# Low parts of value and output weights added up by DMA, and the modulations taken out of the first folded part, in a two-layer decoder trunk

## The chip, the cores and the metric

One core of one Trainium2 chip runs the whole program. The metric is the device time of one execution in microseconds, as the median of the timed runs. TensorE (PE) multiplies, VectorE (DVE), ScalarE (ACT) and GpSimd (POOL) work on tiles of 128 partitions, and SyncE (SP) does nothing but issue DMAs, in the order of its queue.

## The reference

```python
for i in range(DEPTH):                                   # DEPTH = 2, D_MODEL = 1024, SEQ = 512
    mod = silu(c) @ ada_w[i] + ada_b[i]                  # 6 x 1024 modulations
    sh_t, sc_t, gt_t, sh_f, sc_f, gt_f = split(mod, 6)
    h = rmsnorm(x, norm_tok_g[i]) * (1.0 + sc_t) + sh_t
    y = retention_mixer(h, ...) if i % 2 == 0 else mlstm_mixer(h, ...)
    x = x + gt_t * y
    h = rmsnorm(x, norm_ffn_g[i]) * (1.0 + sc_f) + sh_f
    x = x + gt_f * conv_ffn(h, ...)                      # (silu(a) * b) @ w_down, a, b = conv(h @ w_up), D_FF = 2816
return rmsnorm(x, final_g)
```

Both mixers have four heads. A head projects `h` to queries, keys, values (512 wide) and gates, weighs its scores (retention by a fixed decay table, mLSTM by a row that comes from the gates), attends, normalises its result over the 512 values, and multiplies it by the output weights into `x`. All of it is float32.

## The kernel before, in words

`x` and `h` are held transposed, as 8 tiles of 128 features x 512 positions. A float32 product is made of three products of TensorE's reduced type: high x high, high x low and low x high (`mm3`, lines 281 to 283). So every chunk of weights, 128 x 1024 float32 or 512 KB, is loaded by SyncE into a raw buffer `raw` (`Chunk`, line 182; six buffers, `RAWS`), ScalarE casts its high part `whi` (line 164), and VectorE subtracts to get the low part `wlo` (line 169). Both have eight buffers (`WBUFS`). The raw buffer comes free when the low part is made, and only then can SyncE's queue pass the load that takes this buffer next: it is the sixth `raw` load after it.

`low_part_added` (lines 172 to 177) is another way to the low part: ScalarE writes -`whi` into `wlo` (line 175), and a DMA that GpSimd issues adds the raw chunk to it (line 176). Then VectorE has no part in it, and the raw buffer is free once the DMA has landed. Before, only the folded part of the FFN uses it: for the chunk `wa`, the sums `ws` and every second `wt`, 86 DMAs in the two layers.

The program is a list of items (a projection, a piece of attention, a norm), each with the chunks that it uses (`Use`). The last loop of `trunk` goes through it: ahead of each item it loads, casts and splits the chunks of up to four items further on (`Ahead`), then emits the item, then some side work. A scheduler places the instructions on the engines' queues; each queue, SyncE's included, then runs in order. For each layer the items are those of `heads` (line 876): the projections of a head's queries and keys, its values (`v_items`, four chunks a head), its scores (S), gates (g) and attention (A), the middle and the end of its normalisation, and its output pieces (`pieces`, `contract_items`, four chunks a head), with the heads interleaved. `boundary` (line 629) takes the last output pieces in two halves of the positions, with the next norm beside them; then follows the FFN.

What the heads need besides weights comes over SyncE's queue too: the retention's decay table `tab` (line 1091) and the mLSTM's rows `mb` and `db` (lines 1307 and 1308). From `mb` VectorE and ScalarE make the weights of the scores (lines 1314 to 1318).

The FFN's upper part is `folded`, 17 folds in a written order, one `unit(i)` each: products of TensorE with the work for the next unit between them, and the down projection of earlier groups, whose chunks (`Beside`, line 199) lie in two side buffers.

Side work are the modulations: `gemv` (line 136) loads a tile `ada` of 128 x 1025 into one of the two side buffers (line 139), and one VectorE operation multiplies and sums it (line 140). 48 of them run behind the items of mixer 0, as far as `LATER` allows, eight inside the folded part of layer 0 (load at line 525, operation in the next unit), and the others behind every second item later.

Of the kernel before, what the change touches and what calls it, by code (L numbers as in the profile page):

```python
# [15 lines left out]
P = 128  # L16
T = 512
# [11 lines left out]
RAWS = 6  # L29
LATER = 32  # L30
FOLD_FROM = 5
WPAD = 64
OFF = 16
# [37 lines left out]
def trunk(ctx: ExitStack, tc: tile.TileContext, xT, cb, pos, vec, decay, zmask, ada, w_s0, w_in0, w_v0,  # L71
          w_o0, w_in1, w_v1, w_o1, w_up, w_dn, out):
    nc = tc.nc
# [105 lines left out]
    class Chunk:  # L179
# [6 lines left out]

        def low(self):
            self.lo = low_part(self.raw, self.hi, self.r, self.off)

# [162 lines left out]
    class Use:  # L352


        def __init__(self, src, n, off=0):
            self.src, self.n, self.first, self.off = src, n, None, off

# [8 lines left out]
    class Ahead:  # L366
# [26 lines left out]
        def low(self):  # L393
            self.flat[self.at_low].chunk.low()
            self.at_low += 1
# [12 lines left out]

    def folded(folds, h, terms, pairs, downs, modulate):

        no = lambda *a: None
        banks, sums, other = {}, {}, []

# [24 lines left out]
        def unit(i):  # L440
# [50 lines left out]
            if f:  # L491
                f.high_24()
                f.low_24(i % 2)
                if other:
                    layer, m, after, raw = other.pop()
                    gemv(layer, m, raw)
                    after()
            else:
                ahead.high()
                ahead.high()  # L500
# [20 lines left out]
            load_down(i + 2)  # L521
            if modulate and side and i % 2 == 0 and i + 2 < len(folds):
                layer, m, after = side.pop(0)
                raw = aside("ada")[:]
                nc.sync.dma_start(raw, ada[layer, m])
                other.append((layer, m, after, raw))
            if i == len(folds) - 2:
# [42 lines left out]
    def v_items(w_v, hd, h, v, split, between=lambda j: None):  # L570
        pss = []

        def mk(j):
            def fn(w):
                if j == 0:
                    pss.extend(bank("pv") for _ in range(4))
                for t in range(4):
                    for kk in range(2):
                        k = 2 * j + kk
                        cs, ws = slice(t * P, t * P + P), slice(kk * T, kk * T + T)  # L580
                        st, sp = k == 0, k == KT - 1
                        PE.matmul(pss[t][:], h[k].hi[:, cs], w[0].hi[:, ws], start=st, stop=False)  # L582
                        PE.matmul(pss[t][:], h[k].hi[:, cs], w[0].lo[:, ws], start=False, stop=False)  # L583
                        PE.matmul(pss[t][:], h[k].lo[:, cs], w[0].hi[:, ws], start=False, stop=sp)  # L584
                if j == 3:
                    for t in range(4):
                        split(v, pss[t])
            return fn
        for j in range(4):
            item([Use(w_v[hd, j], 2 * T)], mk(j))  # L590
            between(j)
# [22 lines left out]
    def pieces(src, n, gate, ys):  # L614
# [3 lines left out]
        def piece(i):  # L618
            def run(w, t0, t1, after=lambda m: None, js=None, lead=False):
                contract_tiles(w, n, gate, ys, i, t0, t1, after, js, lead)  # L620
            return Use(src(i), per * n * P), run
        return [piece(i) for i in range(KT // per)]
# [6 lines left out]
    def boundary(late, last, norm):  # L629


        for u, _ in late + last:
            u.off = OFF
        for p, after in ((0, lambda m: norm.square(0, m)), (1, norm.later)):
# [280 lines left out]
    class Ffn:  # L915
# [77 lines left out]
        def items(self, norm):  # L993
# [3 lines left out]
            downs = [p for gi in range(len(GROUPS) - 1) for p in self.down(gi)]  # L997
            steps, run = folded(folds, self.h, self.start.terms, pairs, downs, self.layer == 0)

# [398 lines left out]
    for n, (uses, fn, free) in enumerate(items):  # L1398
# [7 lines left out]
        if n < bars[0]:  # L1406
            for _ in range(2 if n > 20 and n % 10 == 0 else 1):
                if len(side) > LATER:
                    side_work(*side.pop(0))
# [107 lines left out]
```

## Time and profile before

| | us |
|---|---|
| median of 3 timed runs | 1559.96 (1559.96 to 1562.13) |
| the profiled execution | 1554.46 |
| its span in the profile | 1552.7 |
| TensorE's granted clock, mean | 0.992 |

Busy shares of the span are 97% for TensorE, 77% for VectorE, 55% for ScalarE and 15% for GpSimd; the DMA engines moved 241.79 MB, 156 GB/s in the mean.

How to read the lines further down: a group gives line, engine, operation, output <- inputs, the number of instructions, then their busy time, the mean ns of one, and the engine's idle time ahead of them with what ended most of it. A line of the waits gives who waited for whom, the sum in us, how often, and the longest. A line of the chain or of a timeline gives start and duration in us, the engine, the line and the tile; "SPq" is SyncE's queue, which stands for the issue of a DMA. Times count from the start of the span.

### The profile page before, as it was taken

How to read it: one execution, taken by the hardware profiler on the slowest of the kernel's cores; microseconds unless marked ns; L12 is line 12 of the kernel's file. 1: busy time of each engine (PE TensorE's matmuls, PEld its weight loads, DVE VectorE, ACT ScalarE, POOL GpSimd, SP SyncE). 2: the span in 40 equal slices, each digit the busy share in tenths (PEclk: the TensorE clock that was granted, in tenths of full speed). 3: DMA queues.
4: the chain of work that ended last, by engine and by line, in shares of the span. 5: the costliest groups of instructions: out<-in, count | busy, mean ns of one | idle time of the engine just before them, and what ended most of it. 6: DMA issues, size and time to landing. Idle time of an engine off the chain costs nothing. (4 is left out here: it accounts for less than half of the span.)

```text
span 1552.7 us, 23173 instructions
## 1 busy us (share of the span) xinstructions
PE 1513.2 (97%) x8996; PEld 1337.2 (86%) x8996; DVE 1200.5 (77%) x1814; ACT 861.2 (55%) x1282; POOL 229.3 (15%) x242
## 2 busy tenths in 40 slices
PE   7999999999999999999999999999999999999997
PEld 4788888888988999998988878888889889999997
DVE  8985768786997878887777777777588977787775
ACT  4534524443456767676655554554545666767763
POOL 3421001110130111111110011001022201111102
PEclk9999999999999999999999999999999999999999
DMA  8753464655315888887444433443312258777751
GB/s 312 228 186 109 143 188 159 204 177 167 110 42 136 210 208 205 230 195 202 160 128 149 149 109 105 152 144 112 126 54 72 67 135 198 195 191 188 187 140 55
DMA packets 72224, 241.79 MB, mean 156 GB/s; under 512 B 9761, under 2 KB 12065, under 8 KB 72114
## 3 DMA queue, kind: packets, MB, share of 16 engines
q1 hardware_dynamic: 59730, 195.22, 38.4%
q0 software_dynamic: 12384, 45.09, 15.3%
q8 instruction: 70, 1.15, 0.3%
q14 instruction: 40, 0.33, 0.1%
HBM read 193.06 MB, written 2.12 MB: 126 GB/s over the span
## 5 line engine op out<-in xcount | busy, mean ns | idle before, releaser
L164 ACT CAST whi<-raw 128x1024 fp32r<-128x1024 f32 (+1 forms) x190 | 194.3, 1029 | 144.4 <-PE pp L282 58.3
L169 DVE TENSOR_TENSOR wlo<-raw,whi 128x1024 fp32r<-128x1024 f32 (+1 forms) x158 | 191.5, 1219 | 46.7 <-ACT whi L164 46.1
L281 PE MATMUL pp<-hh,whi 128*128 128x512 f32 x560 | 218.4, 390 | 2.3 <-DVE vl L278 2.0
L282 PE MATMUL pp<-hl,whi 128*128 128x512 f32 x560 | 218.1, 390 | 0.0
L283 PE MATMUL pp<-hh,wlo 128*128 128x512 f32 x560 | 218.0, 389 | 0.0
L595 DVE SCALAR_TENSOR_TENSOR x<-po,mod,x 128x512 f32<-128x512 f32 (+1 forms) x184 | 114.2, 629 | 71.6 <-PE po L283 68.0
L282 PE MATMUL po<-ggl,whi 128*128 128x512 f32 (+1 forms) x448 | 154.0, 345 | 0.0
L283 PE MATMUL po<-ggh,wlo 128*128 128x512 f32 (+1 forms) x448 | 153.5, 344 | 0.0
L281 PE MATMUL po<-ggh,whi 128*128 128x512 f32 (+1 forms) x448 | 153.0, 345 | 0.0
L422 PE MATMUL p<-hh,whi 128*128 128x256 f32 x544 | 150.6, 277 | 0.0
L423 PE MATMUL p<-hl,whi 128*128 128x256 f32 x544 | 150.4, 276 | 0.0
L424 PE MATMUL p<-hh,wlo 128*128 128x256 f32 x544 | 150.4, 276 | 0.0
L140 DVE SCALAR_TENSOR_TENSOR ada<-ada,c_ext 128x1025 f32<-128x1025 f32 x93 | 115.7, 1245 | 32.3 <-DMA ada<-ada 32.2
L281 PEld LDWEIGHTS pp<-hh,whi 128*128 128x128 f32 x560 | 105.2, 188 | 24.6 <-DVE vl L278 2.5
L283 PEld LDWEIGHTS pp<-hh,wlo 128*128 128x128 f32 x560 | 105.2, 188 | 21.8
L282 PEld LDWEIGHTS pp<-hl,whi 128*128 128x128 f32 x560 | 105.2, 188 | 21.4
L281 PE MATMUL po<-yh,whi 128*128 128x256 f32 (+1 forms) x352 | 115.8, 329 | 0.0
L282 PE MATMUL po<-yl,whi 128*128 128x256 f32 (+1 forms) x352 | 115.6, 328 | 0.0
L283 PE MATMUL po<-yh,wlo 128*128 128x256 f32 (+1 forms) x352 | 115.6, 328 | 0.0
L927 ACT ACTIVATE cv<-p,vecs 128x512 f32<-128x512 f32 x68 | 53.1, 780 | 96.2 <-PE p L424 57.3
L932 DVE SCALAR_TENSOR_TENSOR cv<-p,vecs,cv 128x511 f32<-128x511 f32 (+1 forms) x136 | 101.0, 745 | 2.2
L422 PEld LDWEIGHTS p<-hh,whi 128*128 128x128 f32 x544 | 102.2, 188 | 0.1
(287 smaller groups left out, 3986.9 us busy)
## 6 DMA issues: line engine op xcount, KB each, us to landing
ada<-ada SPq DMA_DIRECT2D x96, 512.5 KB, 4.0
raw<-w_in SPq DMA_DIRECT2D x62, 512.0 KB, 3.8
wb<-w_up SPq DMA_DIRECT2D x34, 512.0 KB, 4.4
wa<-w_up SPq DMA_DIRECT2D x34, 512.0 KB, 5.3
wlo<-wa POOLq DMA_DIRECT2D x34, 512.0 KB, 4.6
wlo<-ws POOLq DMA_DIRECT2D x34, 512.0 KB, 4.9
raw<-w_o SPq DMA_DIRECT2D x32, 512.0 KB, 3.5
raw<-w_dn SPq DMA_DIRECT2D x32, 512.0 KB, 4.4
```

What stands on the lines that cost most here:

```text
L140: return V.scalar_tensor_tensor(raw, raw, 1.0, c_ext[:], op0=ALU.mult, op1=ALU.mult, accum_out=mods[layer][:, f : f + 1])
L164: A.copy(hi, w[:, r])
L169: V.tensor_tensor(lo, w[:, r], hi.bitcast(F32), op=ALU.subtract)
L281: PE.matmul(o, ah, bh, start=start, stop=False)
L282: PE.matmul(o, ah, bl, start=False, stop=False)
L283: PE.matmul(o, al, bh, start=False, stop=stop)
L422: PE.matmul(o, hi[:, ch], b[0], start=st, stop=False, skip_group_check=True)
L423: PE.matmul(o, hi[:, ch], b[1], start=False, stop=False, skip_group_check=True)
L424: PE.matmul(o, lo[:, cl], b[0], start=False, stop=sp, skip_group_check=True)
L595: V.scalar_tensor_tensor(x[m][:, r], ps[:, r], gate_col, x[m][:, r], op0=ALU.mult, op1=ALU.add)
L927: A.activation(acc[:], ps[:], AF.Identity, bias=col("fcb", self.layer * 2 * FT + f), scale=self.conv_col(f, 2))
L932: V.scalar_tensor_tensor(acc[:, s:], ps[:, : T - s], self.conv_col(f, j), acc[:, s:], op0=ALU.mult, op1=ALU.add)
```

## The change

It does three things.

1. The values' chunks (`w_v0` of heads 1 to 3, all of `w_v1`) and the output pieces (`w_o0`, `w_o1`) get `added`, and their low parts are made by `low_part_added`. The pieces inside `boundary` don't. That is 12 + 16 + 2 x 10 = 48 chunks.
2. The eight modulations inside the folded part of layer 0 go, with the code for them.
3. `LATER` is 24 rather than 32, and every fifth item beyond the 20th rather than every tenth has two modulations behind it, so that mixer 0 takes 56 of them.

```diff
--- before.py
+++ after.py
@@ -27,7 +27,7 @@
 WCOLS = 1024
 WBUFS = 8
 RAWS = 6
-LATER = 32
+LATER = 24
 FOLD_FROM = 5
 WPAD = 64
 OFF = 16
@@ -184,8 +184,8 @@
         def high(self):
             self.hi = high_part(self.raw, self.r, self.off)
 
-        def low(self):
-            self.lo = low_part(self.raw, self.hi, self.r, self.off)
+        def low(self, added=False):
+            self.lo = (low_part_added if added else low_part)(self.raw, self.hi, self.r, self.off)
 
         def lo_at(self, at, k):
             return at * P
@@ -352,8 +352,8 @@
     class Use:
 
 
-        def __init__(self, src, n, off=0):
-            self.src, self.n, self.first, self.off = src, n, None, off
+        def __init__(self, src, n, added=False, off=0):
+            self.src, self.n, self.first, self.off, self.added = src, n, None, off, added
 
     def item(uses, fn, free=True):
         for u in uses:
@@ -391,7 +391,8 @@
             self.at_high += 1
 
         def low(self):
-            self.flat[self.at_low].chunk.low()
+            u = self.flat[self.at_low]
+            u.chunk.low(u.added)
             self.at_low += 1
     ahead = Ahead()
 
@@ -406,12 +407,12 @@
             then(ps)
         item([Use(src, KT * P)], fn)
 
-    def folded(folds, h, terms, pairs, downs, modulate):
+    def folded(folds, h, terms, pairs, downs):
 
 
 
         no = lambda *a: None
-        banks, sums, other = {}, {}, []
+        banks, sums = {}, {}
 
         def product(i, n, o, start=False):
             hi, hc, lo, lc = folds[i].p[n]
@@ -491,10 +492,6 @@
             if f:
                 f.high_24()
                 f.low_24(i % 2)
-                if other:
-                    layer, m, after, raw = other.pop()
-                    gemv(layer, m, raw)
-                    after()
             else:
                 ahead.high()
                 ahead.high()
@@ -519,11 +516,6 @@
             if i + 2 < len(folds):
                 folds[i + 2].load()
             load_down(i + 2)
-            if modulate and side and i % 2 == 0 and i + 2 < len(folds):
-                layer, m, after = side.pop(0)
-                raw = aside("ada")[:]
-                nc.sync.dma_start(raw, ada[layer, m])
-                other.append((layer, m, after, raw))
             if i == len(folds) - 2:
                 for _ in range(4):
                     ahead.load()
@@ -587,7 +579,7 @@
                         split(v, pss[t])
             return fn
         for j in range(4):
-            item([Use(w_v[hd, j], 2 * T)], mk(j))
+            item([Use(w_v[hd, j], 2 * T, True)], mk(j))
             between(j)
 
     def add_residual(ps, m, gate_col, t0=0, t1=T):
@@ -618,7 +610,7 @@
         def piece(i):
             def run(w, t0, t1, after=lambda m: None, js=None, lead=False):
                 contract_tiles(w, n, gate, ys, i, t0, t1, after, js, lead)
-            return Use(src(i), per * n * P), run
+            return Use(src(i), per * n * P, n == 4), run
         return [piece(i) for i in range(KT // per)]
 
     def contract_items(ps, between=lambda i: None):
@@ -630,7 +622,7 @@
 
 
         for u, _ in late + last:
-            u.off = OFF
+            u.off, u.added = OFF, False
         for p, after in ((0, lambda m: norm.square(0, m)), (1, norm.later)):
             for n, (u, run) in enumerate(late):
                 item([u], lambda w, run=run, p=p, n=n: run(w[0], *HALVES[p], lead=p + n == 0), False)
@@ -995,7 +987,7 @@
             folds = [Fold((w[f], w[f + FT])) for f in range(FOLD_FROM, FT)]
             pairs = [self.steps(f) for f in range(FOLD_FROM, FT)]
             downs = [p for gi in range(len(GROUPS) - 1) for p in self.down(gi)]
-            steps, run = folded(folds, self.h, self.start.terms, pairs, downs, self.layer == 0)
+            steps, run = folded(folds, self.h, self.start.terms, pairs, downs)
 
             def early(n):
                 todo = [steps.pop(0) for _ in range(n)]
@@ -1404,7 +1396,7 @@
         if not uses or not free or n <= 6:
             continue
         if n < bars[0]:
-            for _ in range(2 if n > 20 and n % 10 == 0 else 1):
+            for _ in range(2 if n > 20 and n % 5 == 0 else 1):
                 if len(side) > LATER:
                     side_work(*side.pop(0))
         elif side and n % 2:
```

In the order of the instructions VectorE has 48 `wlo` subtractions less, ScalarE 48 `ACTIVATE wlo<-whi` more, GpSimd 48 `DMA wlo<-raw` more, and SyncE the same number of DMAs, 61 of them at another place. TensorE's instructions are the same ones in nearly the same order. On SyncE's queue `tab` of retention's head 0 moves ahead of the fourth w_o0 load, which it stood behind; `tab` of head 3 stands behind the load of a w_o0 chunk that takes the buffer of an added one; and the loads of two more modulations come shortly before the first boundary.

**Head 1 of the mLSTM mixer.** First SyncE's queue, where `mb` and `db` of this head stand behind two w_v1 loads; in rows "raw" and a number is a load into a raw buffer. Before:

```order
L182 DMA raw_1663_9314<-w_in1 128x1024
L182 DMA raw_1669_9351<-w_in1 128x1024
L139 DMA ada_1657_9276<-ada 128x1025
L182 DMA raw_1681_9381<-w_v1 128x1024
L182 DMA raw_1693_9461<-w_v1 128x1024
L1307 DMA mb_1577_8886<-scratch_575 128x512
L1308 DMA db_1578_8887<-scratch_575 128x512
```

and after:

```order
L182 DMA raw_1663_9348<-w_in1 128x1024
L139 DMA ada_1627_9128<-ada 128x1025
L182 DMA raw_1669_9385<-w_in1 128x1024
L139 DMA ada_1657_9310<-ada 128x1025
L182 DMA raw_1681_9415<-w_v1 128x1024
L182 DMA raw_1693_9496<-w_v1 128x1024
L1299 DMA mb_1577_8916<-scratch_575 128x512
L1300 DMA db_1578_8917<-scratch_575 128x512
```

The load raw_1693 takes the buffer of raw_1633 in both, the sixth load ahead of it and the fourth w_o1 chunk of head 0. `mb` stands right behind it in both; a modulation's load has moved between the two w_in1 loads. What makes that buffer free has changed; on GpSimd's queue stand, after the change, `zs` and `zv` (the sums for the normalisation of head 0) and the DMAs of the four w_o1 chunks:

```order
L832 TENSOR_TENSOR zs_1536_8728<-z_1529_8681,z_1531_8696 128x512
L833 TENSOR_TENSOR zs_1537_8729<-z_1533_8711,z_1535_8726 128x512
L176 DMA wlo_1619_9064<-raw_1617_9060 128x1024
L176 DMA wlo_1624_9098<-raw_1622_9094 128x1024
L176 DMA wlo_1630_9135<-raw_1628_9131 128x1024
L832 TENSOR_TENSOR zv_1555_8822<-zq_1551_8814,zq_1552_8816 128x512
L833 TENSOR_TENSOR zv_1556_8823<-zq_1553_8818,zq_1554_8820 128x512
L176 DMA wlo_1635_9169<-raw_1633_9165 128x1024
```

Before, the two `zv` rows followed the `zs` rows directly, and no DMA stood on this queue here. The fourth DMA, of raw_1633, now has both `zv` sums ahead of it.

**A little later on VectorE**, where the normalisation of head 0 ends (`grs` is the root of the variance, `z` the head's result, `yl` a low part of what goes into the output product). Before:

```order
L296 RECIPROCAL grs_1605_8975<-grs_1605_8975 128x512
L1355 TENSOR_TENSOR z_1529_8652<-z_1529_8652,grs_1605_8975 128x512
L1355 TENSOR_TENSOR z_1531_8667<-z_1531_8667,grs_1605_8975 128x512
L1355 TENSOR_TENSOR z_1533_8682<-z_1533_8682,grs_1605_8975 128x512
L1358 SCALAR_TENSOR_TENSOR yl_1607_8981<-z_1529_8652,vecs_108,yh_1606_8980 128x512
L1355 TENSOR_TENSOR z_1535_8697<-z_1535_8697,grs_1605_8975 128x512
L1358 SCALAR_TENSOR_TENSOR yl_1609_8986<-z_1531_8667,vecs_108,yh_1608_8985 128x512
L169 TENSOR_TENSOR wlo_1671_9355<-raw_1669_9351,whi_1670_9353 128x1024
```

and after:

```order
L296 RECIPROCAL grs_1605_9005<-grs_1605_9005 128x512
L169 TENSOR_TENSOR wlo_1671_9389<-raw_1669_9385,whi_1670_9387 128x1024
L1347 TENSOR_TENSOR z_1529_8681<-z_1529_8681,grs_1605_9005 128x512
L1347 TENSOR_TENSOR z_1531_8696<-z_1531_8696,grs_1605_9005 128x512
L1347 TENSOR_TENSOR z_1533_8711<-z_1533_8711,grs_1605_9005 128x512
L1350 SCALAR_TENSOR_TENSOR yl_1607_9011<-z_1529_8681,vecs_108,yh_1606_9010 128x512
L1347 TENSOR_TENSOR z_1535_8726<-z_1535_8726,grs_1605_9005 128x512
```

The low part wlo_1671 of a w_in1 chunk, which stood behind the four `z` rows, now stands ahead of them, right behind `grs`.

**The end of the folded part of layer 0, SyncE's queue.** `wa` and `wb` are the last folds' chunks, "raw" of w_dn04 those of the down projection of the last group. Before:

```order
L525 DMA ada_1243_6941<-ada 128x1025
L222 DMA wb_1242_6938<-w_up 128x1024
L223 DMA wa_1241_6937<-w_up 128x1024
L139 DMA ada_1420_8073<-ada 128x1025
L182 DMA raw_1263_7104<-w_dn04 128x768
L182 DMA raw_1264_7106<-w_dn04 128x768
L182 DMA raw_1265_7108<-w_dn04 128x768
L139 DMA ada_1431_8140<-ada 128x1025
L182 DMA raw_1266_7110<-w_dn04 128x768
```

and after:

```order
L222 DMA wb_1219_6793<-w_up 128x1024
L223 DMA wa_1218_6792<-w_up 128x1024
L139 DMA ada_1420_8099<-ada 128x1025
L222 DMA wb_1243_6963<-w_up 128x1024
L223 DMA wa_1242_6962<-w_up 128x1024
L139 DMA ada_1431_8166<-ada 128x1025
L182 DMA raw_1263_7126<-w_dn04 128x768
L182 DMA raw_1264_7128<-w_dn04 128x768
```

The row of line 525, the load of the last folded modulation, is gone, and both `ada` loads of line 139 now stand ahead of all w_dn04 loads, where the second one stood between them.

## The prediction

> **What bounds the kernel now.** I read the busy times first, then TensorE's waits, then the chain of waits, and then the queues around each wait.
>
> ```profile
> span 1552.7 us, 23173 instructions
> PE 1513.2 (97%) x8996; PEld 1337.2 (86%) x8996; DVE 1200.5 (77%) x1814; ACT 861.2 (55%) x1282; POOL 229.3 (15%) x242
> L169 DVE TENSOR_TENSOR wlo<-raw,whi 128x1024 fp32r<-128x1024 f32 (+1 forms) x158 | 191.5, 1219 | 46.7 <-ACT whi L164 46.1
> ```
>
> TensorE is busy for 1513.2 of 1552.7 us, and the change leaves its products as they are. So all that can be won is its idle time, 39.5 us, and all that can be lost is new idle time or a lower clock. VectorE at 77% is not the bound: less work there pays only where TensorE waits for it. These are those waits (us in total, times, longest); the first start-up waits (line 1175 and its neighbours) the change doesn't touch.
>
> ```profile
> PE pms L291 <- ACT ssh L277: 5.2, 3, 2.0
> PE p L424 <- DMA wlo<-wt: 2.1, 1, 2.1
> PE pp L281 <- DVE vl L278: 2.0, 1, 2.0
> PE pvar L291 <- DVE vl L278: 1.3, 1, 1.3
> PE pav L282 <- DVE sl L278: 0.6, 2, 0.4
> PE pden L291 <- ACT o L1328: 0.5, 1, 0.5
> PE pav L281 <- ACT sh L277: 0.3, 1, 0.3
> ```
>
> No row says that TensorE's projections wait for a `wlo` of value or output weights. That is the first finding: the 48 subtractions that the change takes from VectorE end in time today. The gain can only be indirect, and so can the loss.
>
> **The edits themselves.** 48 subtractions of 1.219 us leave VectorE, 58.5 us. In their place come 48 multiplications on ScalarE and 48 DMAs issued by GpSimd. The folded parts show both today:
>
> ```profile
> 720.13 1.06 ACT L175 ACTIVATE wlo<-whi 128x1024 fp32r<-128x1024 f32 x1
> L176 POOL DMA_DIRECT2D wlo<-wa x34: 850/859/1051, 464.9 to 1487.0; - x34
> DMA to landing us min/median/max: 4.4/4.8/10.2
> ```
>
> ScalarE gets 48 x 1.06 = 51 us (55% becomes 58%), GpSimd 48 x 0.86 = 41 us (15% becomes 17%). Neither becomes a bound. A low part is now ready 1.06 + 4.8 = 5.9 us after its cast, at worst 1.06 + 10.2 = 11.3, where it was 1.22. A chunk is loaded up to four items ahead of its use, and that hides the delay from TensorE. The nearest row is that of the folded parts: of their 86 added chunks (34 `wa`, 34 `ws`, 18 `wt`) one is waited for, 2.1 us. At that rate 48 chunks cost from 0 to 1.2 us; I take zero, since that one DMA has a cause of its own (term 2). Without the cover each would cost about 5. But the raw buffer is held that much longer too, and SyncE's queue is in order: whatever stands behind a load that waits for this buffer is late. That is where I look for the price. The eight modulations that leave the folded part of layer 0 are loads and VectorE operations of 1.2 us, which now stand in mixer 0.
>
> **Term 1, head 1 of the mLSTM mixer: a loss.** The chain of waits (start, duration) of before runs through exactly such a buffer:
>
> ```profile
> 915.13 0.60 DVE zv L842
> 915.73 1.15 DVE wlo L169
> 916.89 0.33 SPq L182
> 917.31 5.69 DMA mb<-scratch
> ...
> 939.67 3.37 DVE grs L296
> 943.06 1.90 DVE z L1355 x3
> ...
> 947.00 1.28 ACT L1328
> 948.29 0.61 ACT o L1328
> 948.94 0.51 PE pden L291
> ```
>
> The `wlo` of 915.73 is that of the fourth w_o1 chunk. Its end frees the buffer for the w_v load (raw_1693 in the order), and directly behind that load in SyncE's queue stands `mb`, the row that head 1's score weights need. All that follows up to `pden` is serial, and `pden` already waits 0.5. After the change this chunk is one of the added ones. What sets its DMA:
>
> ```profile
> 912.98 1.05 ACT L164 CAST whi<-raw 128x1024 fp32r<-128x1024 f32 x1 [1.41 <-PE pv L584]
> 910.51 1.30 POOL L840 TENSOR_TENSOR zv<-zq,zq 128x512 f32<-128x512 f32 x1 [6.27 <-issue]
> 911.77 2.28 POOL L841 TENSOR_TENSOR zv<-zq,zq 128x512 f32<-128x512 f32 x1
> ```
>
> The cast waits for TensorE, so it stays at 912.98 to 914.03. The multiplication ends at 915.1. GpSimd has the two `zv` sums ahead of it (they end at 914.05, and up to 1.7 later, because a multiplication now stands between the squares and two DMA issues ahead of the sums). So the DMA goes out at 915.1 to 915.7 and lands 4.4 to 4.8 later, at 919.5 to 920.5, where the subtraction ended at 916.86: `mb` is 2.7 to 3.7 late, I take 3.2. In VectorE's order the `wlo` of raw_1669 now stands ahead of the `z` products where it stood behind them (946.80 below): 1.2 more before `o`.
>
> ```profile
> 946.80 1.22 DVE L169 TENSOR_TENSOR wlo<-raw,whi 128x1024 fp32r<-128x1024 f32 x1
> 437.00:440.00 3.00, 0.97 (x9) 0.77 (x8) 3.00 (x7) 0.81 (x2) 0.00 (x0) 1.00 0.39 152
> 440.00:444.00 4.00, 4.00 (x24) 4.00 (x23) 3.89 (x6) 1.84 (x5) 1.34 (x2) 0.57 0.00 0
> ```
>
> That is +4.4, a stall of about 5 us. The last two rows are stretches of before (duration, then busy times and counts by engine, then the clock): at the boundary at 437 TensorE idles 2.0, and then runs at a mean clock of 0.57 for 4 us. The lost 43% of 4 us are 1.7 us. The waits of 2.1 (735) and 2.0 (`pp` for `vl`) have no such stretch behind them, so 2 us is the edge, and 5 us should be well past it: +1.7. Bounds: without the late `wlo` and without the clock, with the quickest landing, +2.7; with a landing of 7, a second low stretch and the `wlo`, +9; if VectorE's relief lets the cast and the sums come early, +1 at the least.
>
> The Trainium skill ("TensorE: Matmul & The Clock Gate", Part 1: The HAM clock gate) has the clock fall after one idle window of about 3.4 us. The 2.0-us wait at 437 fell short of that and the clock fell all the same, so here the row decides; by either, 5 us is enough.
>
> The same skill ("DMA: Bandwidth & Descriptors", Anatomy of one DMA, SWDGE path) fits a GpSimd DMA as 2.0 us and the bytes at 436 GB/s; for 512 KB I estimate 3.2 us by that page, against the 4.8 median that lands in this trace. By the page `mb` would be about 1.5 us less late and the whole forecast 1.5 us lower; I keep the row.
>
> **Term 2, the end of the folded part of layer 0: a gain.** TensorE's wait of 2.1 for `wlo<-wt` is that of one DMA:
>
> ```profile
> L176 POOL DMA_DIRECT2D wlo<-wt x1: 859/859/859, 727.2 to 727.2; - x1
> DMA to landing us min/median/max: 4.5/5.2/10.2
> ...
> 727.47 0.33 SPq L139 DMA_DIRECT2D ada<-ada  x1
> 729.70 9.58 SPq L182 DMA_DIRECT2D raw<-w_dn  x5
> ```
>
> Issued at 727.2, it landed after 10.2 us, since a modulation's load of 512 KB went out 0.27 later, and five w_dn loads from 2.5 later. That load waited for the buffer of the last folded modulation (726.2 to 727.4 on VectorE). In the order after the change both `ada` loads stand before the w_dn loads and wait for no folded modulation, so the DMA should land in the median. The wait goes: -2.1; if the w_dn loads alone are enough to slow it, 0.
>
> **Terms 3 to 6, small ones.** (3) Head 0 of retention: `tab` moves ahead of one raw load on SyncE's queue and the wait at its `pav` shrinks, -0.4 of the 0.9 that the two `pav` rows give for heads 0 and 3. (4) Head 3: `tab` there stands behind a raw load whose buffer an added chunk frees, about as in term 1, but with a modulation's load beside it that waits longer today: +0.8, at most +3. (5) The boundary of mixer 0: two more modulations stand shortly before it on VectorE (2 x 1.2 us against 1.9 us idle in 408 to 418, 3.37 and 4.74 busy of 10): +0.5.
>
> ```profile
> 408.00:412.00 4.00, 4.00 (x38) 4.00 (x37) 3.37 (x6) 2.15 (x6) 1.92 (x2) 1.00 0.42 131
> 412.00:418.00 6.00, 5.92 (x52) 5.72 (x51) 4.74 (x13) 3.19 (x8) 0.88 (x1) 1.00 0.37 118
> 782.56 1.21 DVE L169 TENSOR_TENSOR wlo<-raw,whi 128x1024 fp32r<-128x1024 f32 x1
> 785.56 1.21 DVE L169 TENSOR_TENSOR wlo<-raw,whi 128x1024 fp32r<-128x1024 f32 x1
> ```
>
> (6) The boundary before mixer 1: three `wlo` of w_v1 (782.56 to 785.56, the first and last of three) leave VectorE beside the norm, but three multiplications enter ScalarE ahead of its squares: -0.5, from -2 to +1. The `vl` wait of 2.0 at the last value chunk stays (a modulation moves ahead of it, +0.2), and the one of 1.3 nets to zero: four `wlo` less on VectorE, as many multiplications on ScalarE ahead of the casts that `vl` needs.
>
> **Sum:** 4.4 + 1.7 - 2.1 - 0.4 + 0.8 + 0.5 - 0.5 + 0.2 = +4.6. The profiled execution took 1554.46, its span of 1552.7 and 1.76 around it, 5.5 less than the median of the timed runs, 1559.96. 1554.46 becomes 1559.1, and on the median's scale I predict **1564.6**.
>
> **The rivals.**
> (a) VectorE's relief wins, the end on the other side. Its place are the rows in which TensorE waits for `vl` and the norms: the `wlo` of w_v1 stood on VectorE ahead of `vl` and of the norm's sums. If those waits go (2.0 + 1.3, and 2.0 of the 5.2 at `pms`), term 2 and 3 come as above (-2.5), and `mb` is late by 2.7 with no lower clock, the sum is -5.1: 1554.9. It decides from the point at which the relief gives more than the 6.1 of term 1, less 2.5. For it: 58.5 us less on VectorE, the largest edit here. Against it: the same stretches get ScalarE work ahead of the casts that these chains need as well. 23%.
> (b) Both sides cancel: `mb` late by 2.7 and the clock stays, no late `wlo`, the rest as in the sum (-1.5): +1.2, 1561.2. For it: waits of 2.0 and 2.1 that left the clock alone. 28%.
> (c) The forecast, 1564.6. 37%.
> (d) The longer-held buffers hurt in more places: `tab` of head 3 is +3 rather than +0.8, the norm of mixer 0 gets all of the 2.4 us, and term 1 meets a landing near 7 (+2.5): +11.1 or 1571. Against it: before `mb` of heads 2 and 3 the buffer of the load ahead is that of a chunk whose low part VectorE still makes, before and after. 11%.
> (e) The change doesn't do what it says. In the order all 48 chunks have their new rows, and no engine has other work; 1%, at 1560.
>
> **How the numbers follow.** What a measurement can tell from no change is 0.2%, 3.1 us: faster is under 1556.8, slower over 1563.1. (a) is nearly all faster, 0.22; (b) and (e) and the low edge of the forecast are the same, 0.31; the rest, 0.47, slower. The range leaves out the outer part of (d) and the low tail of (a): 1555 to 1571; the forecast's own range is 1561 to 1568.
>
> **What would show it.** Term 1: in the chain of waits of after, `mb` lands near 926 rather than 923 and the step before it is a DMA `wlo`, not a VectorE `wlo`; `pden` waits about 5 us and a stretch of about 0.5 of the clock follows. Term 2: no row `p L424 <- DMA wlo<-wt`. Term 5: the first `pms` wait over 2.0. I am wrong if `mb` is issued at 917 again (its DMA landed early or the buffer wasn't the one), or if the `vl` rows vanish.

## The result and the profile after

| | before | after |
|---|---|---|
| median of the timed runs, us | 1560.15 (1559.96 to 1562.13) | 1577.36 (1576.63 to 1582.02) |
| the profiled execution | 1554.46 | 1577.51 |
| its span | 1552.7 | 1575.4 |

The ratio is 1.0114, with an interval of [1.0093, 1.0135]: 17.2 us slower. The direction was forecast, the size was not: 1564.6 was predicted, and 1577.4 lies outside the range of 1555 to 1571.

The page of after, and below it TensorE's waits that answer to those shown of before (the rows of the start, `pst`, come to 11.0 before and 11.8 after):

```profile
span 1575.4 us, 23311 instructions
PE 1520.0 (96%) x8996; PEld 1339.1 (85%) x8996; DVE 1145.9 (73%) x1766; ACT 908.2 (58%) x1330; POOL 263.8 (17%) x290
```

```profile
...
PE pav L281 <- ACT sh L277: 7.5, 1, 7.5
PE pvar L291 <- DVE vl L278: 5.6, 1, 5.6
PE pms L291 <- ACT ssh L277: 4.2, 3, 2.0
...
PE pp L281 <- ACT vt L550: 2.4, 1, 2.4
PE p L424 <- DVE hl L278: 2.4, 2, 2.0
...
PE pden L291 <- ACT o L1320: 1.5, 1, 1.5
```

VectorE lost 54.6 us of work (1200.5 to 1145.9), as it should, and none of that came back as time. TensorE has the same 8996 matmuls in both traces, so the start of the n-th one in each gives how far after lies behind:

| matmuls of (time in after) | after falls behind by |
|---|---|
| values of retention's head 2 (256 to 263) | +3.7 |
| attention of retention's head 3 (365 to 379) | +10.2 |
| start of the folded part, layer 0 (507 to 514) | +4.0 |
| end of the folded part, layer 0 | -2.4 |
| `pvar` of mLSTM's head 0 (931 to 946) | +6.4 |
| `pden` (970), then `pp` (1042) | +1.1, -0.9 |

With the rest the sum is 22.3; the profiled execution of before lies 5.7 under its median and that of after at its median, so the list shows the places rather than the 17.2 us. The largest, at head 3 of retention, is `pav` waiting 7.5 for the scores. On VectorE ahead of it (an idle time and its cause stand in brackets):

```profile
356.38 1.23 DVE L140 SCALAR_TENSOR_TENSOR ada<-ada,c_ext 128x1025 f32<-128x1025 f32 x1 [4.57 <-DMA ada<-ada]
...
362.65 1.23 DVE L140 SCALAR_TENSOR_TENSOR ada<-ada,c_ext 128x1025 f32<-128x1025 f32 x1 [5.03 <-DMA ada<-ada]
...
363.80 1.22 DVE L169 TENSOR_TENSOR wlo<-raw,whi 128x1024 fp32r<-128x1024 f32 x1
364.94 0.75 DVE L554 SCALAR_TENSOR_TENSOR vl<-vt,vm,vh 128x512 fp32r<-128x512 f32 x1
365.60 1.22 DVE L140 SCALAR_TENSOR_TENSOR ada<-ada,c_ext 128x1025 f32<-128x1025 f32 x1
...
371.69 0.69 DVE L1086 TENSOR_TENSOR sp<-psc,tab 128x512 f32<-128x512 f32 x1 [3.60 <-DMA tab<-decay]
```

VectorE stands idle for modulations' loads, with a low part and `vl` queued behind them, and then for `tab`. Over the whole run it waits 65.4 us for modulations, against 32.2 before. What the late transfers may have in common is in the stretches' last two columns (the DMA engines' busy share, GB/s; the columns ahead are duration, busy times and counts by engine, the clock). Before:

```profile
200.00:320.00 120.00, 119.71 (x550) 100.19 (x549) 89.98 (x130) 44.26 (x64) 16.84 (x16) 1.00 0.57 183
320.00:370.00 50.00, 49.71 (x236) 41.73 (x235) 35.41 (x52) 23.88 (x38) 2.24 (x6) 1.00 0.52 179
870.00:960.00 90.00, 87.21 (x411) 72.12 (x410) 67.19 (x99) 46.00 (x72) 14.55 (x16) 1.00 0.35 107
```

After, with the added chunks' DMAs between 140 and 440 in a second fence:

```profile
200.00:320.00 120.00, 117.57 (x532) 98.19 (x532) 77.81 (x121) 49.04 (x69) 21.15 (x23) 0.99 0.75 225
320.00:370.00 50.00, 45.55 (x208) 37.78 (x206) 28.36 (x43) 25.95 (x37) 7.25 (x12) 0.99 0.90 243
870.00:960.00 90.00, 83.74 (x381) 68.83 (x380) 55.49 (x90) 47.84 (x74) 14.41 (x19) 0.96 0.58 160
```

```profile
L176 POOL DMA_DIRECT2D wlo<-raw x18: 852/862/902, 139.5 to 353.8; - x18
...
DMA to landing us min/median/max: 4.8/7.6/10.1
```

The 16 DMA engines are 0.90 busy at the worst place, and an added chunk lands in 7.6 us there, in mixer 0, rather than the 4.8 that the prediction took from the folded parts (in mixer 1, 860 to 1200, the median is 5.4). The modulations' loads of mixer 0 land in 4.9 rather than 3.6 (medians). The third stretch holds other work in after, which is 15 us behind there; from 884 to 974 the share is 0.47. The queues' rows, of before and then of after (packets, MB, the share of all 16 engines' time), give the price of one:

```profile
q1 hardware_dynamic: 59730, 195.22, 38.4%
q0 software_dynamic: 12384, 45.09, 15.3%
```

```profile
q0 software_dynamic: 19296, 70.26, 23.9%
```

23.9% of 1575.4 less 15.3% of 1552.7 is 139 us, or 2.9 us of all 16 engines for each of the 48 chunks, on top of the plain load, which takes 1.6 (38.4% of 1552.7 for 195.22 MB, times 0.524 MB). An added chunk costs the DMA engines nearly three times what it cost before. The share adds up the time of packets and can pass 1 (1.06 from 733 to 735 before), so it doesn't tell how much the engines could still carry.

### The profile page after: what moved, and what is told of

The parts are those of the page before. It is cut to its first block, busy times and chain, and to the rows that moved or that the text cites. A ratio compares the mean times of both kernels' runs of the same rounds, so it can differ in the third digit from the quotient of the medians.

```text
span 1575.4 us, 23311 instructions
## 1 busy us (share of the span) xinstructions
PE 1520.0 (96%) x8996; PEld 1339.1 (85%) x8996; DVE 1145.9 (73%) x1766; ACT 908.2 (58%) x1330; POOL 263.8 (17%) x290
## 3 DMA queue, kind: packets, MB, share of 16 engines
q1 hardware_dynamic: 59730, 195.22, 37.1%
q0 software_dynamic: 19296, 70.26, 23.9%
## 4 chain that ended last, share of the span: by engine, by line
PE 74%; DVE 15%; DMA 4%; issue 3%; ACT 3%; POOL 1%; SPq 0%; DVEq 0%; ACTq 0%; POOLq 0%
PE p L423 7%; PE po L281 7%; PE po L282 7%; PE po L283 7%; PE p L424 7%; PE p L425 7%; PE pp L281 6%; PE pp L282 6%; PE pp L283 6%; PE pv L574 3%; PE pv L575 3%; PE pv L576 3%; DVE wlo L169 2%; DMA ada<-ada 2%; DVE ada L140 2%
## 5 line engine op out<-in xcount | busy, mean ns | idle before, releaser
L140 DVE SCALAR_TENSOR_TENSOR ada<-ada,c_ext 128x1025 f32<-128x1025 f32 x93 | 116.5, 1260 | 65.7 <-DMA ada<-ada 65.4
L424 PE MATMUL p<-hl,whi 128*128 128x256 f32 x544 | 150.4, 277 | 2.4 <-DVE hl L278 2.4
L175 ACT ACTIVATE wlo<-whi 128x1024 fp32r<-128x1024 f32 x134 | 142.2, 1061 | 2.2
L169 DVE TENSOR_TENSOR wlo<-raw,whi 128x1024 fp32r<-128x1024 f32 (+1 forms) x110 | 131.4, 1200 | 15.4 <-ACT whi L164 15.1
L424 PEld LDWEIGHTS p<-hl,whi 128*128 128x128 f32 x544 | 102.1, 188 | 2.8 <-DVE hl L278 2.8
```

What stands on the lines that cost most here:

```text
L140: return V.scalar_tensor_tensor(raw, raw, 1.0, c_ext[:], op0=ALU.mult, op1=ALU.mult, accum_out=mods[layer][:, f : f + 1])
L169: V.tensor_tensor(lo, w[:, r], hi.bitcast(F32), op=ALU.subtract)
L175: A.mul(lo, hi.bitcast(F32), -1.0)
L424: PE.matmul(o, hi[:, ch], b[1], start=False, stop=False, skip_group_check=True)
```

## The experiments

Each ratio is that to the kernel before on the same chip, whose medians were 1558.4 to 1560.2.

| run | median us | ratio and interval |
|---|---|---|
| e1 added chunks only | 1577.6 | 1.0117 [1.0093, 1.0141] |
| e2 moved modulations only | 1565.3 | 1.0032 [1.0018, 1.0045] |
| e3 change, modulations' operations later | 1577.7 | 1.0110 [1.0083, 1.0137] |
| e4 change, rows on ScalarE's queue | 1572.3 | 1.0075 [1.0059, 1.0091] |
| e5 change without loads | 1555.3 | 0.9971 [0.9959, 0.9982] |
| e6 before without loads | 1548.1 | 0.9926 [0.9911, 0.9941] |
| e7 e3 and e4 together | 1580.0 | 1.0129 [1.0107, 1.0151] |
| e8 change, four w_o1 chunks by VectorE | 1578.0 | 1.0117 [1.0098, 1.0137] |
| e9 e5 and e8 together | 1555.6 | 0.9979 [0.9970, 0.9988] |
| e10 change, three side buffers | 1572.5 | 1.0101 [1.0080, 1.0121] |
| e11 before, three side buffers | 1554.1 | 0.9968 [0.9959, 0.9977] |
| e12 before, seven folded modulations | 1554.6 | 0.9978 [0.9968, 0.9987] |
| e13 added chunks only, without loads | 1553.1 | 0.9962 [0.9947, 0.9977] |
| e14 moved modulations only, without loads | 1551.9 | 0.9954 [0.9940, 0.9967] |
| e15 e11 and e12 together | 1552.1 | 0.9956 [0.9944, 0.9969] |
| e16 e10, modulations' loads by GpSimd | 1575.1 | 1.0103 [1.0089, 1.0117] |
| e17 change, quarter loads | 1559.1 | 1.0001 [0.9990, 1.0012] |
| e18 before, quarter loads | 1550.7 | 0.9951 [0.9935, 0.9966] |

**The parts alone.** e1 takes part 1 of the change and leaves the modulations and `LATER`; e2 is the change with these two lines back:

```diff
-            item([Use(w_v[hd, j], 2 * T, True)], mk(j))
+            item([Use(w_v[hd, j], 2 * T)], mk(j))
-            return Use(src(i), per * n * P, n == 4), run
+            return Use(src(i), per * n * P), run
```

> The 48 chunks are added by DMA, and the modulations stay where they were (LATER 32, eight in the folded part). Theory Q (a modulation's load stands on SyncE's queue behind a raw load that waits for an added chunk's DMA, and its operation then holds VectorE's queue): most of the loss of 17.2 us stays, namely the stalls of head 3 of retention (+10.2 of the profile) and head 1 of mLSTM (+7.3), while the +4.0 at the start of the folded part of layer 0 and the gain of 2.4 at its end go: 1569 to 1576. Theory M (eight more modulations in mixer 0 are too many, the added chunks cost little): under 1564.

> The modulations move as in the change (LATER 24, every fifth item two, none in the folded part), and no chunk of the mixers is added by DMA. Theory Q: the +4.0 at the start of the folded part stays, perhaps some of the +3.7 at head 2's values, and the 2.4 at the end of the folded part are won: 1559 to 1566. Theory M: nearly the whole loss is here, 1570 or more.

The added chunks alone bring the whole loss (+17.4), a little above what was expected, with +9.6 at head 3 of retention and +7.6 at head 1 of the mLSTM mixer in the profile. The moved modulations cost 5.1 alone, and nothing more beside the added chunks. Theory M falls. But the largest stall doesn't need the added chunks: in e2, too, `pav` of retention's head 3 waits 4.4 us, and the list has +7.7 there (in a profile 1.8 us over e2's median), with the DMA engines' share nearly as before:

```profile
320.00:370.00 50.00, 45.40 (x200) 36.63 (x199) 34.54 (x51) 20.59 (x34) 2.24 (x6) 0.97 0.54 182
```

`tab` goes out at 359.7 there, against 352.7 before. Either half of the change brings this stall, and the two don't add up (+9.6 and +7.7 alone, +10.2 together).

**The places in the queues.** e3 emits each modulation's operation one call of side work after its load (`side_done` emits that of the load before); e4 moves three loads:

```diff
     def side_work(layer, f, after):
+        raw = aside("ada")[:]
+        nc.sync.dma_start(raw, ada[layer, f])
+        side_done()
+        waiting.append((layer, f, after, raw))
...
```

```diff
-        nc.sync.dma_start(tab[:], decay[i])
+        nc.scalar.dma_start(tab[:], decay[i])
-        nc.sync.dma_start(mb[:], scratch[i : i + 1].broadcast_to([P, T]))
+        nc.scalar.dma_start(mb[:], scratch[i : i + 1].broadcast_to([P, T]))
...
```

> The change as it is, but each modulation's VectorE operation is emitted one item of side work later than its load, so that the load has an item's time to land. Theory Q: VectorE's waits for modulations (65.4 us after, 32.2 before) fall below 35, the stalls of head 3 of retention and head 1 of mLSTM shrink by half or more: 1569 or less. Theory P (the score rows tab and mb themselves stand behind the raw loads, as the prediction had it for mb; VectorE's waits are beside the point): within 3 us of 1577.4.

> The change as it is, but tab, mb and db are issued on ScalarE's queue instead of SyncE's, so that no raw load stands ahead of them. Theory P: the stall of 7.5 us at pav of retention's head 3 goes with the lower clock behind it (10.2 us), and about 1 at pden of mLSTM's head 1: 1566 or less. Theory Q: VectorE is itself held until 368.1 by modulations and low parts ahead of sp, where tab landed at 371.6, so only 3.6 of that stall go, with some of the clock: 1571 to 1575.

e4's time came as theory Q had it, though `pav` still waits 5.0 of the 7.5. With `tab` in time, what ended last there were the modulations one after the other (the chain of waits of e4):

```profile
342.17 4.42 DMA ada<-ada
346.69 1.25 DVE ada L140 x2
347.96 6.23 DMA ada<-ada
354.21 1.25 DVE ada L140 x2
355.48 5.43 DMA ada<-ada
```

But e3's time was the one that theory P named: VectorE's waits for modulations fell to 44.3 only, TensorE's longest wait at `pav` fell from 7.5 to 1.4 and that at `pvar` from 5.6 to 1.7, and the one at `pden` rose from 1.5 to 6.4; the time stayed. (The expectations count each of these stalls somewhat longer.) So the stalls change places. e7 tested whether the two edits together end that, and e8 whether the four w_o1 chunks of term 1 start it (`u.added = i > 0` for the output pieces of mLSTM's head i).

> The change with both edits of the runs before: each modulation's operation one item of side work later, and tab, mb and db on ScalarE's queue. In the run with the first edit alone the stall before pav fell from 7.7 to 2.4 us, that at pvar from 5.7 to 1.9, and the one at pden rose from 1.7 to 6.6, where mb was late. If these rows take the place of the modulations as the last to come (R and P together), pden falls under 2 too and the time is 1564 to 1570. If something else holds the scores there, it stays near 1577.

> The change, but the four w_o1 chunks of mLSTM's head 0 get their low parts from VectorE again. If these four chunks cause the loss at head 1 of the mLSTM mixer (in the profile +5.4, +0.8 and +1.1), it is gone: 1568 to 1572, with pvar waiting 1.5 as before and mb landing no later than before relative to the scores. If the DMAs of the value chunks or GpSimd's other work cause it, 1575 or more.

Neither edit won anything: e7 stayed near 1577 and e8 over 1575, the second outcome of each text. In e7 `mb`, issued at 931.2 on ScalarE's queue, was first used at 939.8, 8.6 us later, and a modulation held VectorE for 3.7 more in the middle of the scores. In e8 `pden`'s wait was gone, but `pvar` still waited 4.6 and the time was that of the change. No single place in a queue carries the loss.

**Without the loads.** In e5 and e6 the modulations beside the items load nothing; e13 and e14 do the same to the parts, and e9 adds e8's edit.

```diff
-        tc.keep_in_program_order(gemv(layer, f, raw))
+        tc.keep_in_program_order(V.scalar_tensor_tensor(aside("ada")[:], c_ext[:], 1.0, c_ext[:], op0=ALU.mult,
+                                                        op1=ALU.mult, accum_out=mods[layer][:, f : f + 1]))
```

> The change, but the modulations that run beside the items load nothing: the 80 loads are left out, and their VectorE operations stay in place and multiply another tile, so the output is not the reference's. Theory R (a ring: a modulation's load stands on SyncE's queue behind a raw load that waits for an added chunk, it waits for its side buffer too, and its operation holds VectorE's queue, low parts and scores behind it): without the loads no ring, the stalls before pav of retention's head 3 and pvar of mLSTM's head 0 (7.7 and 5.7 us after) fall under 2 each, and the time is within 4 us of the next kernel. Theory S (the added chunks' slow landings hold the raw loads, and GpSimd's sums stand behind their issues, with or without modulations): both stalls stay over 4, and the time is 8 or more above the next kernel.

> The kernel before with the same loads left out (72 of them; the eight in the folded part stay), the measure for the run ahead; its output is not the reference's either. Both theories: between 1556 and 1561, since before no long wait hangs on these loads except the last one of the folded part.

> The change without the 80 modulation loads (they are left out, so the output is not the reference's), and the four w_o1 chunks of mLSTM's head 0 get their low parts from VectorE again. Beside the run with the loads alone left out (1555.3; 7.1 above the kernel before without them, of which its profile shows +4.0 at pden of mLSTM's head 1): if mb is late there since it stands behind the load that takes the buffer of one of these four chunks, as term 1 had it, those 4 go: 1550 to 1552.5. If the late mb has another cause: 1554 or more.

> The added chunks alone (modulations as before), and the 72 loads of modulations beside the items are left out, so the output is not the reference's. Without these loads the kernel before took 1548.1 and the change 1555.3. If the added chunks alone cost nothing once no modulation's load stands among their raw loads (the loss of 17.4 of the added chunks alone is all of the ring): 1548 to 1550. If they carry the 7.1 that are left: 1553 to 1556.

> The moved modulations alone, without the 80 loads, so the output is not the reference's. If the 7.1 that are left between the change and the kernel before come from the VectorE operations of the surplus modulations at the start of the folded part: 1550 to 1553 (its profile showed 2.2 there). If they cost only by their loads: 1546 to 1549, the 2.4 of the folded part's end won.

Without these loads the change is 7.1 above the kernel before, not 17.2, and the delay at `pav` is 1.1 rather than 10.2: 10 of the 17 us need the modulations' loads. Both stalls fell under 2 as theory R had it (0.6 at `pav`, 1.9 at `pvar`), but 7.1 lies between the ranges of R and S. The 7.1 come from both parts: +5.0 for the added chunks alone (e13), +3.8 for the moved modulations alone (e14), a little more than 7.1 in sum, on another chip than e5 and e6. e6 came out below its range: in the kernel before, too, these loads cost 12 us. e9 took 1555.6, the outcome for another cause of the late `mb`; its profile has 4.1 us less at `pden` than that of e5, and 2.6 more ahead of it, and the medians are the same, so term 1's wait isn't shown to cost anything by itself.

**Buffers and the queue.** e10 and e11 have a third side buffer; e16 issues the modulations' loads from GpSimd as well.

```diff
-NSLOTS = 55
+NSLOTS = 53
-    asides = ctx.enter_context(tc.tile_pool(name="asides", bufs=2))
+    asides = ctx.enter_context(tc.tile_pool(name="asides", bufs=3))
```

```diff
-            nc.sync.dma_start(raw, ada[layer, f])
+            nc.gpsimd.dma_start(raw, ada[layer, f])
```

> The change with three side buffers in place of two (and 53 in place of 55 general slots, to make room). If the wait of a modulation's load for its side buffer is a link of the ring (ring by the buffer), VectorE's waits for modulations fall from 65 us to under 45 and the time to 1566 to 1573. If the loads are late only because they stand behind raw loads on SyncE's queue (ring by the queue alone), 1574 or more.

> The kernel before with three side buffers and 53 general slots, the measure for the run ahead, and a try at a better version: the kernel before without modulation loads was 12 us faster, so the waits for them cost something there too. If the buffer is the link, 1552 to 1558; if the queue alone is, or two general slots are missed, 1559 to 1565.

> The change with three side buffers, and the modulations' loads issued by GpSimd in place of SyncE, so that no raw load stands ahead of them; the order of nearly everything else is that of the run with three side buffers alone (1572.5, with the stalls of 5.7 at pav's place and 5.2 at pden's in the sum of its profile). If SyncE's queue is the link (ring by the queue): 1558 to 1565. If GpSimd's queue, which now holds both these loads and the added DMAs, or the added chunks' own landings hold the same stretches: 1570 or more.

e10 came inside the range for a ring by the buffer, with VectorE's waits for modulations down to 30.6. But a third buffer takes 4.3 us from the kernel before as well, so the loss between the two stays (18.4): these waits don't carry it. In e16 no raw load stands ahead of a modulation's, and it is about as slow as the change, so SyncE's queue alone isn't the link. A ring through GpSimd's queue isn't excluded: there the modulations' loads waited 99.0 us for VectorE's operations between 140 and 440, with added chunks' DMAs behind them.

**The bytes.** e17 and e18 keep every load, its place and its waits, and take three quarters of the bytes away; the product's operand is another tile, so that VectorE's time stays.

```diff
+        raw = aside("ada")[:]
+        nc.sync.dma_start(raw[:, :256], ada[layer, f][:, :256])
+        tc.keep_in_program_order(V.scalar_tensor_tensor(raw, c_ext[:], 1.0, c_ext[:], op0=ALU.mult, op1=ALU.mult,
+                                                        accum_out=mods[layer][:, f : f + 1]))
```

> The change, but each modulation beside the items loads a quarter of its bytes (256 of 1025 columns; the rest of the load and of the product is left out, so the output is not the reference's). Every load stands where it stood, waits for its side buffer and for the raw loads ahead, and its operation takes as long and waits for it. Theory D (the 16 DMA engines are full: their busy share in 320 to 370 of the profile is 0.90 after and 0.52 before, and the rows land late for that): nearly as quick as with no loads (1555.3): 1555 to 1562, and 7 to 10 above the next kernel. Theory R (the places in the queues make the loads late, whatever their size): 1567 or more, 13 or more above the next kernel.

> The kernel before with the same quarter loads, the measure for the run ahead; the output is not the reference's. Without the loads it took 1548.1. Theory D: 1548 to 1551. Theory R: 1552 or more, the places in the queues being those of the kernel before.

Both came as theory D had it: 1559.1 and 1550.7, 8.4 apart. With all places in the queues as they were, fewer bytes take 9 of the 17 us away. In the profiles most of it is at `pav`, where e17 falls behind e18 by 2.1 rather than 10.2; of the 6.4 at `pvar` 3.7 are left, and of the 4.0 at the start of the folded part 3.3. The stretches of e17 that were 0.75 and 0.90 after:

```profile
200.00:320.00 120.00, 120.00 (x552) 100.58 (x551) 82.24 (x127) 52.30 (x72) 23.70 (x24) 1.00 0.55 148
320.00:370.00 50.00, 49.42 (x232) 40.85 (x231) 30.81 (x47) 27.98 (x42) 5.93 (x11) 1.00 0.68 184
```

At 0.68 TensorE is busy for 49.42 of the 50 us, at 0.90 for 45.55. And the added chunks, whose bytes are those of after, land earlier (the DMAs of their line between 140 and 440 in e17; 7.6 in the median after, and 5.3 in e5, which has no such loads):

```profile
DMA to landing us min/median/max: 4.7/5.8/7.7
```

So in mixer 0 the loads and the added chunks slow each other on the engines that they share. In mixer 1 (860 to 1200) the added chunks land in 6.0 in e17 and 5.4 in after, and no such effect shows. One rival stands: a quarter load is also over sooner by itself (2.2 us in e18, 3.6 before), which shortens every chain of waits that runs through such loads. Against this as the whole reason, VectorE waits longer for modulations in e17 (38.9) than in e10 (30.6), which keeps the loss; no run separates the two. A high share alone doesn't do it, either. The folded part of layer 0 has run at 0.83 all along, in the kernel before too:

```profile
510.00:700.00 190.00, 190.00 (x1358) 177.06 (x1357) 154.44 (x247) 136.09 (x185) 28.39 (x33) 1.00 0.83 208
```

TensorE doesn't idle there: its chunks are loaded two units ahead, in a written order. In the mixers a load that lands late meets a queue of VectorE or SyncE that stands behind it, as the lines of 356 to 372 show.

**A better version.** e12 takes the last modulation out of the folded part; e15 joins it with e11's edit.

```diff
-            if modulate and side and i % 2 == 0 and i + 2 < len(folds):
+            if modulate and side and i % 2 == 0 and i + 4 < len(folds):
```

> The kernel before with the last of the eight folded modulations taken out of the folded part (seven are left; the eighth runs beside a later item). Term 2 as predicted: the load that collided with the last wt DMA no longer goes out there, the wait of 2.1 at p is gone, and nothing else changes: 1557 to 1558.5. If the w_dn loads alone slow that DMA: 1560.

> The kernel before with three side buffers (53 general slots) and seven folded modulations in place of eight, the two edits that gave 1554.1 and 1554.6 alone. If their gains add up (4.3 and 3.8): 1549 to 1552. If both remove the same waits: 1553 to 1555.

e12 gained 3.8, more than its range had, of which its profile has 2.4 at the end of the folded part. e15 is 7 us faster than the kernel before, by the ratio 0.9956 [0.9944, 0.9969], the best version with nothing left out; the two gains nearly add up. It has one load fewer where they collide, and a third buffer gives each load more time.

## Why the prediction was wrong

- **Direction and sign:** right, slower, but in part by luck: the sum was slower through term 1, which e8 and e9 don't bear out as the cause.
- **The edits themselves: this step failed.** It added up ScalarE's 51 us and GpSimd's 41 and found that "neither becomes a bound"; it took an added chunk's transfer as a delay of 4.8 us, hidden at a cost of zero, and never as work of the DMA engines. It is 139 us of all 16 of them, put into mixers that kept them 0.35 to 0.57 busy, beside modulations and raw loads. The added chunks alone cost 17.4 us (e1), and with a quarter of the modulations' bytes the loss of the change halves (e17 with e18). The moved modulations, too, were priced as VectorE's time (term 5, +0.5), not as loads on SyncE's queue; alone they cost 5.1 (e2).
- **Term 4 was mis-sized, and its wait is another one.** It has the right place and +0.8, at most +3, where the profile shows +10.2. It took `tab` to be late behind the raw load that takes an added chunk's buffer. The chain of after:

```profile
364.94 0.75 DVE vl L554
365.69 1.15 DVE ada L140 x2
367.28 4.31 DMA tab<-decay
371.69 0.70 DVE sp L1086
373.08 0.80 PE pav L281
```

  `tab` goes out at 367.28 behind a modulation's load, issued at 366.86, whose side buffer VectorE's operation had just left. It landed in 4.3 us, no slower than before (5.6): it was issued late. The chain to it runs through loads that landed late (4.9 for 3.6 in the median) and operations that waited for them. e4 shows that `tab`'s place is not the whole of it, and e2 that added chunks aren't needed for a stall here.
- **Term 1:** 6.1 were forecast for head 1 of the mLSTM mixer and 7.4 measured, at `pvar` and `pden` together, but not as written, so that the near size is luck. The chain of after:

```profile
930.27 1.26 POOL zv L833
931.53 9.08 DMA wlo<-raw
941.08 4.15 DMA mb<-scratch
```

  `mb` does stand behind the DMA of this chunk, as forecast, with a landing of 9.08 rather than 4.4 to 4.8. But the long wait is at `pvar`, 5.6, since VectorE waited 6.0 for a modulation ahead of `zv`, and e8 kept the loss without these four added chunks. The mechanism was there; it isn't shown to be the cause.
- **The clock:** right in kind. Behind both long stalls TensorE runs at about half (0.50 and 0.55 in the stretches of after below); by these rows about half of 6 us and 0.45 of 5 us are lost, an estimate of 3.0 and 2.3, where +1.7 was the price for one.

```profile
373.00:379.00 6.00, 5.92 (x13) 3.50 (x14) 5.47 (x12) 2.09 (x5) 0.00 (x0) 0.50 0.00 0
...
938.00:943.00 5.00, 5.00 (x14) 3.89 (x14) 1.40 (x3) 0.23 (x1) 0.00 (x0) 0.55 0.88 303
```

- **Term 2:** right, -2.4 for -2.1; no `p L424 <- DMA wlo<-wt` is left. **Term 3:** -0.8 for -0.4. **Terms 5 and 6:** +0.3 for +0.5, -0.4 for -0.5.
- **Missing:** +4.0 at the start of the folded part. It is there in e2 too and not in e1: the surplus modulations, which mixer 0 has no items for, pile up behind it (VectorE has five of them between 480 and 520 in after, one before). The profile of e14 has 2.6 of it without any load, so that much is VectorE's time and order there. The +3.7 at head 2's values are in neither part at that size (+1.2 in e1, none in e2) and not in e5; so they need the loads and both parts; more isn't shown.
- **Rivals:** (d) came nearest, with longer-held buffers that hurt in more places, at 11% and 1571; it, too, had no DMA engines in it. (a) is refuted: VectorE's 54.6 us bought nothing.

What stays open: how much of the 9 us that e17 wins is the sharing of the engines, and how much the shorter loads; and why mixer 1 loses at `pvar`, where the added chunks land hardly later than in the folded parts. Of the 5.0 us that the added chunks cost without any modulation's load (e13), the profile of e5 shows parts at `pvar` and `pden`, but e9 did not win them back. What makes an added chunk land in 8.6 us at a share of 0.75 (200 to 320 in after) where those of the folded part at 0.83 land in 5.7 (medians), no run separates; the transfers may come in denser bunches there.

The Trainium skill's fit for a GpSimd DMA ("DMA: Bandwidth & Descriptors", Anatomy of one DMA, SWDGE path) gave an estimate of 3.2 us for 512 KB. The measured median was 4.8 in the folded parts and 7.6 in mixer 0, so here the row decides. The 2.9 us of all 16 engines per chunk are not a landing time, and stand beside it.

## What to carry to other kernels

A DMA that does an engine's arithmetic is work for the DMA engines: multiply its count by its share of their time, and look up that share in the very stretch where it will run, as you would for any engine. An engine that is 77% busy and off the path has nothing to sell, while here more bytes on DMA engines that were half busy made loads late, and where in-order queues stood behind these loads, stalls came of it. When stalls change places from edit to edit, look for the resource that they share and take its load away with all places kept, rather than move one more instruction; and say what else the lighter load changes.

## What the runs showed of the hardware

- A DMA of 512 KB that adds to its target took 2.9 us of the 16 DMA engines, a plain load of 512 KB from HBM 1.6.
- Transfers of one kind lengthened those of another in mixer 0: the added chunks landed in 7.6 us beside the modulations' full loads, 5.8 beside a quarter of their bytes, and 5.3 beside none (medians). The share by itself doesn't tell how late: 8.6 at 0.75, 5.7 at 0.83.
